# The Overflow branch's copies issued by GpSimd, and four conditioning chunks computed by GpSimd and ScalarE

## The chip, the cores and the metric

The kernel runs on one NeuronCore of a Trainium2 chip. The time is that of one execution on the device, in microseconds (us). Five engines run their own instruction queues and meet through semaphores: TensorE (PE in the profile; PEld are its weight loads), VectorE (DVE), ScalarE (ACT), GpSimd (POOL) and SyncE (SP). Sixteen DMA engines move the data; here SyncE issues nearly all loads of weights.

## The reference

One sequence of 256 tokens of width 1024 goes through nine stages: attention, a mixture of experts, a pooling mixer, a second mixture of experts, a final norm, and then four more blocks (mixer_ab, a feed-forward block, mixer_c, a second feed-forward block). All is f32. The first part conditions each layer on one vector `c`:

```python
c_act = silu(c)
for i in range(DEPTH):                       # 2
    mod = c_act @ ada_w[i] + ada_b[i]        # (1024) x (1024, 6144)
    sh_m, sc_m, gt_m, sh_f, sc_f, gt_f = split(mod, 6)
    h = modulate(rmsnorm(x, norm_mix_g[i]), sh_m, sc_m)
    y = fox_attention(h, ...) if i == 0 else pool_mixer(h, ...)
    x = x + gt_m * y
    h = modulate(rmsnorm(x, norm_ffn_g[i]), sh_f, sc_f)
    y = grouped_moe(h, router_w, router_bias, w1[i], w3[i], w2[i])   # 32 experts, 2 per token
    x = x + gt_f * y
```

An expert is `(silu(x @ w1) * (x @ w3)) @ w2` with a hidden width of 512; each token goes to two of 32 experts.

## The kernel before

**Weights.** All large weights come in chunks of 128 x 4096 f32 (2.097 MB). `prefetch` (L206) issues them on SyncE's queue, strictly in the order of a list, each into a slot of one of three rings: ringa with three slots, ringb with four (until the second mixture of experts is done), ringc with three (opened after attention, closed in layer 1's expert loop). A chunk is issued when a slot is free, that is when `free` has been called for the chunk that was in it; on the chip SyncE then waits for the engine that reads that chunk last.

**Conditioning.** The product of `c_act` with `ada_w` is 24 chunks, ADA, of 4 x 1024 x 128 numbers each. The first four and the last four are multiplied by TensorE. The sixteen between, ADA_ROWS = ADA[4:20], are VectorE's, in `ada_cols` (L657): the chunk lies with 128 output columns on the partitions, and for each of its four groups one instruction multiplies 128 x 1024 weights by `crow` (c_act on every partition), adds them up along the row and adds the bias (L663; in the trace it is CUSTOM_DVE_ANT_0 with a READ_ACCUMULATOR behind it). `attention` calls `ada(2)` whenever a weight chunk of its own is used up, so that the chunks are spread over the stage; the loads of attn, ada and wo chunks follow the same order. `gate` and update of the residual x (L761) come at the end of attention.

**Experts.** Each mixture of experts runs over 16 pairs p of experts. Per pair: `up` (64 matmuls of L1190 with four weight chunks), silu and product (L1194, L1197), `turned` (four transposes L1203 and the copy into the tile uT, L1205), `down` (32 matmuls L1217 with two chunks, then the result in two parts into the tiles yh and yl: L1228 and L1229 in layer 0, L1223 to L1226 in layer 1), and `spread_out` (L1237, L1242) of the pair before. `gather` (L1155) fetches the tokens of the next two pairs with the one-hot oh (L1141), and gate products (L1144) follow. A pair has room for 64 tokens of each expert.

**Overflow.** If an expert gets more tokens than that, `overflow` redoes its share with a loop. It is called in both layers at p = 9, between `up` and `turned`, and it is an If on a number that the engines load from `mint` (L1287, L1288). It borrows the buffers hg, oh, uT, yh and yl. In the run shown no expert overflows, so the branch is skipped. The copies within it (one, and 26 in the body of a loop, L1299 to L1325) are issued by ScalarE. Transfers that the hardware queues of SyncE and ScalarE issue are counted on eight semaphores, DMAHW0 to DMAHW7, in turn; those that GpSimd issues on DMASW0 to DMASW7. Where a branch is skipped, the program raises the counts by what the branch would have added.

**What sets the order.** TensorE's order is written out by hand (manual schedule). On the other engines a scheduler orders the instructions by its own estimate of when they are ready.

Of the kernel before, what the change touches and what calls it, by code (L numbers as in the profile page):

```python
# [19 lines left out]
T = 256  # L20
# [19 lines left out]

ADA = [(l, j) for l in range(2) for j in range(12)]
ADA_ROWS = ADA[4:20]

VEC = {}
_n = 0
# [119 lines left out]
class Net:  # L165
# [491 lines left out]
    def ada_cols(self, l, j):  # L657
# [7 lines left out]
        self.free(("ada", l, j))  # L665
        self.ada_done(l, j)

    def ada_mm(self, chunks, row, pp, tags=("pL", 2, "gm", 1)):

        nc = self.nc  # L670
        n = len(chunks)
        pg = pp.tile([128, 512], F32, name=tags[0], bufs=tags[1])
        ws = [self.get(("ada",) + a).rearrange("p (k n) -> p k n", k=KT) for a in chunks]
        for kt in range(KT):
            for i, w in enumerate(ws):
                q = 32 * (kt % 4 if n == 1 else 2 * i + kt % 2)
                nc.tensor.matmul(pg[q:q + 32, :], self.ca[:, kt:kt + 1].to_broadcast([128, 32]), w[:, kt, :], start=kt < 4 // n, stop=kt >= KT - 4 // n)
        for a in chunks:
            self.free(("ada",) + a)
        nc.scalar.copy(row, pg)  # L680

        def turn():
            pm = pp.tile([128, n, 4], F32, name=tags[2], bufs=tags[3])
            for c in range(4):
                nc.tensor.matmul(pm[:, :, c], row[:, c * 128:(c + 1) * 128], self.sel if n == 1 else self.halfsel,
                                 start=True, stop=True)
            for i, (l, j) in enumerate(chunks):
                nc.vector.tensor_tensor(self.mod[l][:, 4 * j:4 * j + 4], pm[:, i, :], self.vec(f"ada_b{l}", 4 * j, 4), op=OP.add)
                self.ada_done(l, j)
        return turn  # L690
# [10 lines left out]
    def attention(self):  # L701
        nc, tc = self.nc, self.tc
        with ExitStack() as es:
# [63 lines left out]

            def ada(n):
                for _ in range(n):
                    self.ada_cols(*todo.pop(0))  # L770

            lo, hi = range(0, 4), range(4, 8)
            qk(0, 0, range(4))
# [504 lines left out]
    def overflow(self, l, htok, gate, slot, mint, cap, yacc, wp, pp):  # L1278


        nc, tc, A = self.nc, self.tc, self.A
        h = wp.tile([128, KT, T], F32, name="hg")
        idr = wp.tile([128, 2, 4, 64], F32R, name="oh").rearrange("p a b n -> p (a b n)")[:, 0:128]
        ug = wp.tile([128, 4, 128], F32, name="uT").rearrange("p a n -> p (a n)")
        u, gr = ug[:, 0:T], ug[:, T:2 * T]
        w, wd = (wp.tile([128, D], F32, name=n) for n in ("yh", "yl"))
        rv = nc.values_load(mint[0:1, 0:1], min_val=0, max_val=T)  # L1287
        with tc.If(rv > cap):  # L1288
            with ExitStack() as es:
                dp = es.enter_context(tc.tile_pool(name=f"ovd{l}", bufs=1, space=DRAM))  # L1290
                rows = dp.tile([NE, T], F32, name="rows")
                nc.scalar.copy(idr, self.ident)
                ov, rsb = w[:, 0:2 * NE].rearrange("p (a e) -> p a e", a=2), wd[0:NE, 0:T]
                nc.vector.scalar_tensor_tensor(ov, slot, float(cap), gate, op0=OP.is_gt, op1=OP.mult)
                pr = pp.tile([NE, T], F32, name="e1", bufs=2)
                for tt in range(2):
                    nc.tensor.transpose(pr[:, tt * 128:(tt + 1) * 128], ov[:, tt, :], self.ident)
                nc.vector.tensor_copy(rsb, pr)
                nc.scalar.dma_start(rows, rsb)  # L1299
                for k in range(KT):  # L1300
                    ph = pp.tile([128, T], F32, name="e1", bufs=2)
                    for tt in range(2):
                        for i in range(2):
                            nc.tensor.matmul(ph[:, tt * 128:(tt + 1) * 128], htok[i][:, tt, k * 128:(k + 1) * 128], idr,
                                             start=i == 0, stop=i == 1)
                    nc.vector.tensor_scalar(h[:, k, :], ph, self.mscale[l][:, 1, k:k + 1], self.shift(l, 1)[:, k:k + 1],
                                            op0=OP.mult, op1=OP.add)
                wk = w.rearrange("p (k n) -> p k n", k=KT)
                we = A["exp"][l].rearrange("q c p (a b n) -> q c p a b n", a=4, b=2)
                with tc.For_i(0, NPAIR, 1) as pv:  # L1310
                    for ab in range(2):
                        src = rows[:, :].rearrange("(q a) t -> q a t", a=2)[ds(pv, 1), ab, :]
                        nc.scalar.dma_start(gr, src.to_broadcast([128, T]))
                        for ft in range(4):
                            ps = []
                            for i in range(2):
                                for c in range(2):
                                    nc.scalar.dma_start(
                                        wk[:, 4 * c:4 * c + 4, :],
                                        we[ds(pv, 1), 2 * i + c, :, :, ab, ft * 128:(ft + 1) * 128]  # L1320
                                        .rearrange("q p a n -> (q p) a n"))
                                ps.append(pp.tile([128, T], F32, name="e0", bufs=2))
                                self.dense(ps[i], wk, 0, h)
                            for hf in range(2):
                                nc.scalar.dma_start(wd[:, 512 * hf:512 * hf + 512],  # L1325
                                                  we[ds(pv, 1), 4 + hf, :, ft, ab, :].rearrange("q p n -> (q p) n"))
                            nc.scalar.activation(u, ps[0], AF.Silu)
                            nc.vector.tensor_tensor(u, u, ps[1], op=OP.mult)
                            nc.vector.tensor_tensor(u, u, gr, op=OP.mult)
                            if l:  # L1330
                                nc.vector.tensor_tensor(wd, wd, self.gb, op=OP.mult)
                                for tt in range(2):
                                    for hf in range(2):
                                        nc.tensor.matmul(yacc[tt][hf], u[:, tt * 128:(tt + 1) * 128], wd[:, 512 * hf:512 * hf + 512],
                                                         start=False, stop=False, skip_group_check=True)
                            else:
                                for nt in range(KT):
                                    nc.tensor.matmul(yacc[:, nt, :], wd[:, nt * 128:(nt + 1) * 128], u,
                                                     start=False, stop=False, skip_group_check=True)
# [1078 lines left out]
```

## Time and profile before

| | us |
|---|---|
| median of 3 runs | 1869.39 |
| lowest and highest | 1868.79, 1871.61 |
| the profiled execution | 1871.96 |
| its span (first to last instruction) | 1870.2 |
| attention, to the last update of x | about 192 |
| mixture of experts of layer 0, to its last `down` | 677.3 |
| mixture of experts of layer 1, to its last `down` | 1186.5 |

The page gives busy times of the engines and the span in 40 slices with the DMA rate. The timeline lists instructions with start, length and, in brackets, the idle time of their engine before them and what ended it: `[5.78 <-SPq L1288]` is a wait of 5.78 us that SyncE's instruction of line 1288 ended. The list of waits adds these up. The windows give busy times, the granted clock of TensorE as a share of 2.4 GHz (PEclk) and the busy share of the DMA engines.

### The profile page before, as it was taken

How to read it: one execution, taken by the hardware profiler on the slowest of the kernel's cores; microseconds unless marked ns; L12 is line 12 of the kernel's file. 1: busy time of each engine (PE TensorE's matmuls, PEld its weight loads, DVE VectorE, ACT ScalarE, POOL GpSimd, SP SyncE). 2: the span in 40 equal slices, each digit the busy share in tenths (PEclk: the TensorE clock that was granted, in tenths of full speed). 3: DMA queues.
4: the chain of work that ended last, by engine and by line, in shares of the span. 5: the costliest groups of instructions: out<-in, count | busy, mean ns of one | idle time of the engine just before them, and what ended most of it. 6: DMA issues, size and time to landing. Idle time of an engine off the chain costs nothing. (4 is left out here: it accounts for less than half of the span.)

```text
span 1870.2 us, 26586 instructions
## 1 busy us (share of the span) xinstructions
PE 1738.4 (93%) x11262; PEld 1165.4 (62%) x11262; DVE 791.0 (42%) x1552; ACT 532.7 (28%) x950; POOL 163.6 (9%) x249
## 2 busy tenths in 40 slices
PE   6998999999589989999995999999999999999998
PEld 4666544443234445444433434779999989989997
DVE  4687422211112125222522242665655566565554
ACT  2321211111001122111200101445644466564443
POOL 0000000000000000000440340223000002200000
PEclk9999999999789999999997999989999999999999
DMA  9998899999999996999996999615344533344531
GB/s 397 426 422 317 366 427 427 426 428 426 426 390 426 426 428 273 421 426 410 427 426 273 421 413 426 256 68 193 150 177 180 196 143 136 136 158 181 214 127 66
DMA packets 41665, 582.52 MB, mean 311 GB/s; under 512 B 4625, under 2 KB 4753, under 8 KB 5953
## 3 DMA queue, kind: packets, MB, share of 16 engines
q1 hardware_dynamic: 41328, 580.46, 75.1%
q8 instruction: 92, 1.51, 0.3%
q10 hardware_dynamic: 208, 0.26, 0.1%
q14 instruction: 37, 0.30, 0.0%
HBM read 579.65 MB, written 1.05 MB: 311 GB/s over the span
## 5 line engine op out<-in xcount | busy, mean ns | idle before, releaser
L243 DVE TENSOR_TENSOR wlo<-ringa,whi 128x1024 fp32r<-128x1024 f32 x192 | 228.5, 1231 | 174.6 <-ACT whi L242 174.6
L1190 PE MATMUL e<-ringb,hg 128*64 128x512 f32 x1056 | 233.9, 594 | 1.2 <-DMA ringb<-in_exp 1.2
L242 ACT CAST whi<-ringa 128x1024 fp32r<-128x1024 f32 x192 | 191.4, 1050 | 144.2 <-issue 54.9
L266 PE MATMUL ph<-hlo,whi 128*128 128x256 f32 x704 | 198.8, 282 | 1.2 <-DVE hlo L557 1.2
L265 PE MATMUL ph<-hhi,whi 128*128 128x256 f32 x704 | 198.6, 282 | 0.0
L267 PE MATMUL ph<-hhi,wlo 128*128 128x256 f32 x704 | 198.4, 282 | 0.0
L1197 DVE TENSOR_TENSOR u<-u,e 128x512 f32<-128x512 f32 x32 | 22.0, 688 | 384.1 <-PE e L1190 384.1
L1190 PEld LDWEIGHTS e<-ringb,hg 128*64 128x64 f32 x1056 | 79.6, 137 | 146.2 <-issue 141.8
L1190 PE MATMUL e<-ringa,hg 128*64 128x512 f32 x592 | 134.2, 599 | 17.7 <-DVE yl L1229 16.0
L266 PEld LDWEIGHTS ph<-hlo,whi 128*128 128x128 f32 x704 | 133.9, 190 | 2.4 <-DVE hlo L557 1.6
L265 PEld LDWEIGHTS ph<-hhi,whi 128*128 128x128 f32 x704 | 133.9, 190 | 0.8
L267 PEld LDWEIGHTS ph<-hhi,wlo 128*128 128x128 f32 x704 | 133.9, 190 | 0.0
L1467 POOL TENSOR_TENSOR ringa<-ringa 128x128 f32<-128x128 f32 (+1 forms) x86 | 45.8, 545 | 813.5 <-DVE ringa L1463 703.3
L1217 PE MATMUL e<-ringa,uT 128*64 128x512 f32 x384 | 91.4, 623 | 19.4 <-DVE uT L1205 15.8
L1190 PEld LDWEIGHTS e<-ringa,hg 128*64 128x64 f32 x592 | 45.1, 138 | 100.9 <-issue 81.7
L1217 PE MATMUL e<-ringb,uT 128*64 128x512 f32 x416 | 95.8, 606 | 8.8 <-DVE uT L1205 7.2
L1190 PE MATMUL e<-ringc,hg 128*64 128x512 f32 x400 | 88.4, 592 | 1.8 <-DMA ringc<-in_exp 1.8
L1228 ACT ACTIVATE yh<-e,gs 128x512 fp32r<-128x512 f32 x32 | 21.9, 687 | 226.0 <-PE e L1217 195.3
L1160 ACT ACTIVATE hg<-e,mod,msc 128x256 f32<-128x256 f32 x64 | 36.2, 565 | 164.9 <-DVE hg L1162 157.1
L1224 ACT CAST yh<-u 128x512 fp32r<-128x512 f32 x32 | 19.8, 618 | 217.6 <-DVE u L1223 217.6
L1155 PE MATMUL e<-oh,hth 128*128 128x256 f32 x256 | 68.9, 305 | 12.1 <-DVE oh L1141 7.5
L1229 DVE SCALAR_TENSOR_TENSOR yl<-e,gs,yh 128x512 fp32r<-128x512 f32 x32 | 23.9, 750 | 123.7 <-ACT yh L1228 123.7
(588 smaller groups left out, 3209.5 us busy)
## 6 DMA issues: line engine op xcount, KB each, us to landing
ringb<-in_exp SPq DMA_DIRECT2D x92, 2048.0 KB, 20.0
ringa<-in_exp SPq DMA_DIRECT2D x61, 2048.0 KB, 19.7
ringc<-in_exp SPq DMA_DIRECT2D x39, 2048.0 KB, 24.0
ringa<-in_f SPq DMA_DIRECT2D x32, 2048.0 KB, 7.5
ringb<-in_ada SPq DMA_DIRECT2D x15, 2048.0 KB, 16.2
ringa<-in_ada SPq DMA_DIRECT2D x9, 2048.0 KB, 21.9
ringa<-in_cin SPq DMA_DIRECT2D x8, 2048.0 KB, 7.4
ringa<-in_attn SPq DMA_DIRECT2D x3, 2048.0 KB, 28.2
```

The costliest lines, as they stand in the source:

```text
L242: nc.scalar.copy(hi[:, o], raw[:, o])
L243: (eng or nc.vector).tensor_tensor(lo[:, o], raw[:, o], hi[:, o], op=OP.subtract)
L265: mm(ps, wh, ah, start=start, stop=False, **kw)
L266: mm(ps, wh, al, start=False, stop=False, **kw)
L267: mm(ps, wl, ah, start=False, stop=stop, **kw)
L1155: nc.tensor.matmul(pd[:, i, :], htok[h][:, tt, k * 128:(k + 1) * 128], oh[:, tt, :], start=tt + h == 0, stop=tt + h == 2)
L1160: nc.scalar.activation(hg[q][:, k, :], pd[:, i, :], AF.Identity, scale=sc[:, k:k + 1], bias=sh[:, k:k + 1])
L1190: nc.tensor.matmul(ps[s, :], h[:, kt, o:o + 64], w[:, k, ab, :], start=kt == 0, stop=kt == KT - 1)
L1197: nc.vector.tensor_tensor(u, u, ph[1], op=OP.mult)
L1217: nc.tensor.matmul(py[s, :], uT[:, ft, s], w[:, ft, ab, :], start=ft == 0, stop=ft == 3)
L1229: nc.vector.scalar_tensor_tensor(lo, py, g, hi, op0=OP.mult, op1=OP.subtract)
L1467: nc.gpsimd.tensor_tensor(o, a, b, op=op)
```

## The change

Two edits. The copies inside `overflow` are issued by GpSimd's queue in place of ScalarE's. And four of VectorE's sixteen conditioning chunks, ADA_POOL = ADA[9:17:2] (numbers 9, 11, 13 and 15), go to a new function: GpSimd multiplies each row by crow in place, ScalarE sums the row along with a copy in place, and GpSimd adds the bias.

```diff
--- before.py
+++ after.py
@@ -40,6 +40,7 @@
 
 ADA = [(l, j) for l in range(2) for j in range(12)]
 ADA_ROWS = ADA[4:20]
+ADA_POOL = ADA[9:17:2]
 
 VEC = {}
 _n = 0
@@ -665,6 +666,18 @@
         self.free(("ada", l, j))
         self.ada_done(l, j)
 
+    def ada_cols2(self, l, j):
+
+        nc = self.nc
+        w = self.get(("ada", l, j)).rearrange("p (n k) -> p n k", n=4)
+        m = self.mod[l][:, 4 * j:4 * j + 4]
+        for n in range(4):
+            nc.gpsimd.tensor_tensor(w[:, n, :], w[:, n, :], self.crow, op=OP.mult)
+            nc.scalar.activation(w[:, n, :], w[:, n, :], AF.Identity, accum_out=m[:, n:n + 1])
+        self.free(("ada", l, j))
+        nc.gpsimd.tensor_tensor(m, m, self.vec(f"ada_b{l}", 4 * j, 4), op=OP.add)
+        self.ada_done(l, j)
+
     def ada_mm(self, chunks, row, pp, tags=("pL", 2, "gm", 1)):
 
         nc = self.nc
@@ -767,7 +780,8 @@
 
             def ada(n):
                 for _ in range(n):
-                    self.ada_cols(*todo.pop(0))
+                    a = todo.pop(0)
+                    (self.ada_cols2 if a in ADA_POOL else self.ada_cols)(*a)
 
             lo, hi = range(0, 4), range(4, 8)
             qk(0, 0, range(4))
@@ -1296,7 +1310,7 @@
                 for tt in range(2):
                     nc.tensor.transpose(pr[:, tt * 128:(tt + 1) * 128], ov[:, tt, :], self.ident)
                 nc.vector.tensor_copy(rsb, pr)
-                nc.scalar.dma_start(rows, rsb)
+                nc.gpsimd.dma_start(rows, rsb)
                 for k in range(KT):
                     ph = pp.tile([128, T], F32, name="e1", bufs=2)
                     for tt in range(2):
@@ -1310,19 +1324,19 @@
                 with tc.For_i(0, NPAIR, 1) as pv:
                     for ab in range(2):
                         src = rows[:, :].rearrange("(q a) t -> q a t", a=2)[ds(pv, 1), ab, :]
-                        nc.scalar.dma_start(gr, src.to_broadcast([128, T]))
+                        nc.gpsimd.dma_start(gr, src.to_broadcast([128, T]))
                         for ft in range(4):
                             ps = []
                             for i in range(2):
                                 for c in range(2):
-                                    nc.scalar.dma_start(
+                                    nc.gpsimd.dma_start(
                                         wk[:, 4 * c:4 * c + 4, :],
                                         we[ds(pv, 1), 2 * i + c, :, :, ab, ft * 128:(ft + 1) * 128]
                                         .rearrange("q p a n -> (q p) a n"))
                                 ps.append(pp.tile([128, T], F32, name="e0", bufs=2))
                                 self.dense(ps[i], wk, 0, h)
                             for hf in range(2):
-                                nc.scalar.dma_start(wd[:, 512 * hf:512 * hf + 512],
+                                nc.gpsimd.dma_start(wd[:, 512 * hf:512 * hf + 512],
                                                   we[ds(pv, 1), 4 + hf, :, ft, ab, :].rearrange("q p n -> (q p) n"))
                             nc.scalar.activation(u, ps[0], AF.Silu)
                             nc.vector.tensor_tensor(u, u, ps[1], op=OP.mult)
```

What moves on the engines. First ScalarE at layer 0's branch, from the hg activations of the next pairs to pair 10's silu; the semaphores that an instruction waits for stand behind it. Before:

```order
L1160 ACTIVATE hg<-e_3055,mod_106,msc_108 128x256 [waits DVE_49]
L1228 ACTIVATE yh<-e_3075,gs 128x512 [waits DMAHW0_49,DMAHW7_49,PE_49,Activation_49]
L1228 ACTIVATE yh<-e_3088,gs 128x512 [waits PE_49]
L1194 ACTIVATE u<-e_3101 128x512 [waits PE_49]
L1228 ACTIVATE yh<-e_3185,gs 128x512 [waits DVE_49,PE_49]
```

and after:

```order
L1174 ACTIVATE hg<-e_3075,mod_106,msc_108 128x256 [waits DVE_49]
L1242 ACTIVATE yh<-e_3095,gs 128x512 [waits DMASW0_49,DMASW7_49,PE_49,Activation_49]
L1242 ACTIVATE yh<-e_3108,gs 128x512 [waits PE_49]
L1208 ACTIVATE u<-e_3121 128x512 [waits PE_49]
L1242 ACTIVATE yh<-e_3205,gs 128x512 [waits DVE_49,PE_49]
```

The order is the same; the first write of yh waits for the software queue's counters in place of the hardware queues'. VectorE at the same place, from the gate products to pair 10's product, before:

```order
L1144 TENSOR_TENSOR oh<-oh,gate 128x256 [waits DVE_49]
L1205 COPY uT<-e_3066 128x512 [waits DMAHW2_49,PE_49]
L1144 TENSOR_TENSOR oh<-oh,gate 128x256 [waits DVE_49]
L1229 SCALAR_TENSOR_TENSOR yl<-e_3075,gs,yh 128x512 [waits DMAHW1_49,DMAHW2_49,DMAHW0_49,Activation_49]
L1229 SCALAR_TENSOR_TENSOR yl<-e_3088,gs,yh 128x512 [waits Activation_49]
```

and after:

```order
L1158 TENSOR_TENSOR oh<-oh,gate 128x256 [waits DVE_49]
L1219 COPY uT<-e_3086 128x512 [waits DMASW2_49,PE_49]
L1158 TENSOR_TENSOR oh<-oh,gate 128x256 [waits DVE_49]
L1243 SCALAR_TENSOR_TENSOR yl<-e_3095,gs,yh 128x512 [waits DMASW1_49,DMASW2_49,DMASW0_49,Activation_49]
L1243 SCALAR_TENSOR_TENSOR yl<-e_3108,gs,yh 128x512 [waits Activation_49]
```

Here too the counters alone are others. GpSimd from the mask at the start to layer 0's branch, before:

```order
L312 TENSOR_SCALAR mask<-jp 128x128 x2
L945 TENSOR_TENSOR rws<-vt,msc_108 128x256
L945 TENSOR_TENSOR rws<-vt,msc_109 128x256
L1287 TENSOR_LOAD mint
L1288 COMPARE_AND_BRANCH
```

and after:

```order
L675 TENSOR_TENSOR ringa<-ringa,crow 128x1024 x4
L678 TENSOR_TENSOR mod_106<-mod_106,vt 128x4
L959 TENSOR_TENSOR rws<-vt,msc_108 128x256
L675 TENSOR_TENSOR ringb<-ringb,crow 128x1024 x4
L678 TENSOR_TENSOR mod_106<-mod_106,vt 128x4
L675 TENSOR_TENSOR ringa<-ringa,crow 128x1024 x4
L678 TENSOR_TENSOR mod_107<-mod_107,vt 128x4
L675 TENSOR_TENSOR ringb<-ringb,crow 128x1024 x4
L678 TENSOR_TENSOR mod_107<-mod_107,vt 128x4
L959 TENSOR_TENSOR rws<-vt,msc_109 128x256
L1301 TENSOR_LOAD mint
L1302 COMPARE_AND_BRANCH
```

Sixteen products and four bias sums stand ahead of the second of the two rws products (the router's weights, scaled). And VectorE at the end of attention, over the last two conditioning chunks, before:

```order
L663 ISA mod_107 128x1
L761 SCALAR_TENSOR_TENSOR x<-pL,mod_106,x 128x256
L663 ISA ringa,mod_107<-ringa,crow,vt 128x1024
L663 ISA mod_107 128x1
L663 ISA ringa,mod_107<-ringa,crow,vt 128x1024
L663 ISA mod_107 128x1
L663 ISA ringa,mod_107<-ringa,crow,vt 128x1024
L663 ISA mod_107 128x1
L761 SCALAR_TENSOR_TENSOR x<-pL,mod_106,x 128x256
L663 ISA ringa,mod_107<-ringa,crow,vt 128x1024
L663 ISA mod_107 128x1
L761 SCALAR_TENSOR_TENSOR x<-pL,mod_106,x 128x256 x4
```

and after:

```order
L664 ISA mod_107 128x1
L774 SCALAR_TENSOR_TENSOR x<-pL,mod_106,x 128x256
L664 ISA ringa,mod_107<-ringa,crow,vt 128x1024
L664 ISA mod_107 128x1
L664 ISA ringa,mod_107<-ringa,crow,vt 128x1024
L664 ISA mod_107 128x1
L664 ISA ringa,mod_107<-ringa,crow,vt 128x1024
L664 ISA mod_107 128x1
L664 ISA ringa,mod_107<-ringa,crow,vt 128x1024
L664 ISA mod_107 128x1
L774 SCALAR_TENSOR_TENSOR x<-pL,mod_106,x 128x256 x4
```

The last chunk's four rows stand in one block, where before an update of x stood between its third and its fourth.

## Rows read from the trace of the kernel before

**Rows 1.** the page: its span, and GB/s moved in its 40 slices

```profile
span 1870.2 us, 26586 instructions
...
GB/s 397 426 422 317 366 427 427 426 428 426 426 390 426 426 428 273 421 426 410 427 426 273 421 413 426 256 68 193 150 177 180 196 143 136 136 158 181 214 127 66
```

**Rows 2.** waits of SyncE, 470 to 560 and 975 to 1060: total, times, longest

```profile
SPq L1288 <- SPq L1288: 38.7, 8, 5.0
...
SPq L1288 <- SPq L1288: 25.2, 1, 25.2
```

**Rows 3.** timeline, layer 0's branch: start, length, engine, line, tiles, idle before

```profile
207.84 0.69 POOL L945 TENSOR_TENSOR rws<-vt,msc 128x256 f32<-128x256 f32 x1 [124.57 <-DVE yh L1087]
471.79 3.65 PE L1190 MATMUL e<-ringb,hg 128*64 128x512 f32 x16 [1.15 <-DMA ringb<-in_exp]
496.54 0.69 DVE L1205 COPY uT<-e 128x512 f32<-128x512 f32 x1 [5.78 <-SPq L1288]
497.29 9.30 PE L1217 MATMUL e<-ringb,uT 128*64 128x512 f32 x32 [7.19 <-DVE uT L1205]
521.01 1.27 ACT L1228 ACTIVATE yh<-e,gs 128x512 fp32r<-128x512 f32 x2 [30.66 <-SPq L1288]
522.54 8.62 PE L1190 MATMUL e<-ringa,hg 128*64 128x512 f32 x32 [15.95 <-DVE yl L1229]
```

**Rows 4.** timeline, layer 1's branch, and the last matmuls of its last `down`

```profile
973.88 3.65 PE L1190 MATMUL e<-ringa,hg 128*64 128x512 f32 x16 [0.17 <-DMA ringa<-in_exp]
1003.60 0.69 DVE L1205 COPY uT<-e 128x512 f32<-128x512 f32 x1 [14.38 <-SPq L1288]
1004.35 6.63 PE L1217 MATMUL e<-ringa,uT 128*64 128x512 f32 x16 [15.78 <-DVE uT L1205]
1010.81 3.60 PE L1217 MATMUL e<-ringb,uT 128*64 128x512 f32 x16
1182.87 3.60 PE L1217 MATMUL e<-ringa,uT 128*64 128x512 f32 x16
```

**Rows 5.** timeline of TensorE, pairs 13 and 15 of layer 0, and its end

```profile
600.61 7.07 PE L1190 MATMUL e<-ringb,hg 128*64 128x512 f32 x32
652.92 7.07 PE L1190 MATMUL e<-ringa,hg 128*64 128x512 f32 x32
670.19 7.09 PE L1217 MATMUL e<-ringc,uT 128*64 128x512 f32 x32
```

**Rows 6.** windows: length, busy us of PE, PEld, DVE, ACT, POOL, PEclk, DMA share, GB/s

```profile
120.00:140.00 20.00, 20.00 (x87) 10.19 (x86) 16.96 (x46) 6.17 (x22) 0.00 (x0) 1.00 1.00 422
500.00:540.00 40.00, 24.05 (x109) 8.70 (x106) 2.10 (x3) 1.86 (x3) 0.00 (x0) 0.76 0.92 383
1000.00:1020.00 20.00, 13.00 (x186) 5.69 (x187) 5.99 (x12) 1.24 (x2) 0.00 (x0) 0.74 0.48 185
```

**Rows 7.** groups by line (last column: busy, mean ns | idle before)

```profile
L663 DVE CUSTOM_DVE_ANT_0 ringb<-ringb,crow,vt 128x1024 f32<-128x1024 f32 x32 | 39.1, 1273 | 0.0
L1911 POOL TENSOR_TENSOR xc<-xc,vt 128x1024 f32<-128x1024 f32 x1 | 2.5, 2455 | 0.0
L242 ACT CAST whi<-ringa 128x1024 fp32r<-128x1024 f32 x192 | 191.4, 1050 | 144.2 <-issue 54.9
```

**Rows 8.** timeline of TensorE at the end of attention: its waits for VectorE

```profile
161.47 3.72 PE L759 MATMUL pL<-oT,ringb 128*128 128x256 f32 x16 [2.34 <-DVE x L761]
169.40 1.13 PE L759 MATMUL pL<-oT,ringb 128*128 128x256 f32 x4 [3.41 <-DVE x L761]
173.41 4.87 PE L759 MATMUL pL<-oT,ringb 128*128 128x256 f32 x12 [2.88 <-DVE x L761]
```

**Rows 9.** timeline around 1244, GpSimd's product and VectorE's scans

```profile
1244.03 2.46 POOL L1911 TENSOR_TENSOR xc<-xc,vt 128x1024 f32<-128x1024 f32 x1
1244.54 2.09 DVE L1711 TENSOR_TENSOR_SCAN wr<-s5mag,wr 128x64 f32<-128x64 f32 x2
1246.87 0.27 DVE L1711 TENSOR_TENSOR_SCAN wr<-s5mag,wr 128x64 f32<-128x64 f32 x1
```

## The prediction

> **What bounds the kernel now.** I read the page first, then busy time by windows, then the waits and the timeline at the two places that the change touches. The span is 1870.2 us [rows 1]; the profiled execution took 1871.96 us, 1.8 us of it outside the span, and the median of the three runs is 1869.39 us, 2.6 us under the profiled one. The sums below are made against the span and then carried to the median. Two limits take turns in the first 1200 us: the weight stream, which moves 426 to 428 GB/s wherever it is not held up [rows 1], and TensorE.
>
> The Overflow branch sits in each layer's expert loop behind the first half of pair 9. It is not taken here, and still costs time. SyncE stands at the branch line for 38.7 us in layer 0 and for 25.2 us in layer 1, released each time by itself, step by step [rows 2]: it raises, one by one, the counters that the skipped copies of the ScalarE queue would have raised, and each raise waits until the earlier loads on that counter have landed. Meanwhile it issues no load, and whoever touches a tile that the branch could have written waits as well. In layer 0 [rows 3] the copy into uT waits 5.78 us for SyncE, TensorE's second half of pair 9 starts 7.19 us late, ScalarE's first write of yh waits 30.66 us for SyncE, and TensorE starts pair 10 at 522.54 us after 15.95 us of waiting. In layer 1 [rows 4] the copy into uT waits 14.38 us and TensorE 15.78 us.
>
> **The change part by part: the copies of the branch.** They move to GpSimd and so to counters of their own (the order rows show uT, yh and yl waiting for DMASW where DMAHW stood). SyncE then has nothing to raise. GpSimd must raise its own counters where the branch is skipped, but no transfer ran on them before, and it comes to layer 0's branch right behind its second rws product, which ran at 207.84 us [rows 3], some 270 us before TensorE does, and to layer 1's behind the products that it makes for the S5 part in pairs before. What stays is each engine's own passage through the branch.
>
> Layer 0. The copy into uT would start 5.8 us earlier, pair 9's second half at 491.5 instead of 497.29, and after its 9.30 us [rows 3] pair 10 at about 501 instead of 522.54. TensorE can't keep all 21.7 us. Two pairs take it 652.92 - 600.61 = 52.31 us [rows 5], 26.2 us each, but a pair needs six chunks of 2.097 MB, 4.91 us each at 427 GB/s, 29.5 us. So it runs into the loads again, three or so pairs before the end. The last chunk of pair 9's first half was in at 471.79, where TensorE began on it as soon as it landed; 38 more chunks follow (two, then six for each of six pairs), the last lands at 471.79 + 38 x 4.91 = 658.4, its 16 matmuls take 3.5, and the layer ends at 661.9. Before it ended at 670.19 + 7.09 = 677.28 [rows 5]. Gain 15.4 us. If the stream still loses what it loses between 500 and 540 now (a DMA share of 0.92 over 40 us, 3.2 us [rows 6]), 12; if the loads were in early enough for TensorE to keep everything, 21.7; the middle one is worked out from this stage's own pace, and I take it.
>
> Behind this layer the router and layer 1's start run with full rings, so the shift is carried along whole.
>
> Layer 1. The first half of pair 9 meets its last load by 0.17 us [rows 4], so the loads are no further ahead there. Without SyncE's steps uT goes 14.4 us earlier, as soon as the gate product in front of it ends. The 32 matmuls of the second half now take from 1004.35 to 1010.81 + 3.60 = 1014.41, 10.06 us, at a granted clock of 0.74 between 1000 and 1020 [rows 6], where the same 32 take 7.09 us at full clock [rows 5]: the clock had been dropped to 1.2 GHz behind the idle stretch. With a gap of about 2 us in its place most of these 3.0 us should come back. 14.4 + 3.0 = 17.4; I take 17. From 1004 on TensorE waits for no load until 1182.87 + 3.60 = 1186.47 [rows 4]. Does that stay so when it starts 17 us earlier? The last of 38 chunks would be in at 973.88 + 38 x 4.91 = 1160.5 and the layer could end at 1164.0; TensorE wants to end at 1169.5. It does, by 5 us. Lower bound 11 (a clock low at the other end, a load that comes late by 3 us), upper 19.
>
> The stretch behind 1187 hangs on TensorE, VectorE and ScalarE handing work to each other, its loads follow TensorE's pace, and nothing of it is edited: shift carried, 0 us.
>
> **The conditioning chunks.** Sixteen of VectorE's multiply-and-sum rows (four chunks of four) leave it, 16 x 1.21 us pitch (1.27 us each [rows 7]) = 19.3 us. Where these stood, TensorE is busy the whole time (20.00 of 20 us [rows 6]): that is cover, and the 19.3 us free nothing by themselves. TensorE waits for VectorE only at the end of attention, 2.34, 3.41 and 2.88 us [rows 8], because the rows of the last four chunks stand between x updates that free TensorE's accumulators. Those four chunks stay on VectorE. In the order rows of after, the last chunk's four stand in one block, where before an update stood between its third and its fourth row: one row, 1.2 us, more ahead of an update that TensorE waits for, and the same once more at the update before if TensorE's place has slipped against VectorE's. I put both, 2 x 1.2 = 2.4 us. The bounds are a gain of 8.6 us (VectorE so far ahead that all three waits go) and the loss below.
>
> GpSimd's price for a 128x1024 product of two tensors is 2.46 us [rows 7], 16 of them 39.4 us; ScalarE's for a 128x1024 pass 1.05 us [rows 7], 16.8 us. GpSimd is idle there. ScalarE's sums stand in its queue ahead of copies and exponentials that TensorE waits for, so a late product holds those too. And the two engines get in each other's way: a pair of small scans on VectorE, 0.27 us for one, took 2.09 us beside GpSimd's 2.46 us product, and ended 0.14 us behind it [rows 9]. A VectorE row with two SBUF inputs that comes upon a running product waits for its end. The moved products meet VectorE's other chunk rows, which have two such inputs. If half of the 16 are met halfway, 8 x 1.2 = 9.8 us, less than the 19.3 taken off; I put 1 us on the path. Attention: 2.4 + 1 = 3.4 us longer. If every product holds VectorE for its whole length, 39.4 - 19.3 = 20.1 us longer. The end of attention is where SyncE's stream takes up again, and TensorE meets loads until pair 9, so the shift is carried.
>
> The Trainium skill says this too: the page "GPSIMD Engine Reference" (sections "Specifications" and "Key points") has GpSimd and VectorE share their SBUF interfaces, with contention for VectorE instructions that have two SBUF inputs. By that rule, taken at its worst, the time would be that of the second rival below; the trace shows the contention [rows 9], but only for single instructions.
>
> **Sum.** 1870.2 - 15.4 - 17 + 3.4 = 1841.2 us of span, 1843.0 for an execution like the profiled one, 1840.4 against the median. Forecast 1840 us, in its own range 1834 to 1848.
>
> **The rivals.** (a) Attention gains: VectorE's 19.3 us put it so far ahead that the three waits vanish. 8.6 us less instead of 3.4 more: 1828. For it: all three are for VectorE [rows 8]. Against: the rows in the tail are as many as before, in larger blocks. Chance 0.10.
>
> (b) Products hold VectorE each time, 20.1 us instead of 3.4: 1857. For it, [rows 9]; against, much of VectorE's work between its chunk rows has one input in PSUM (the score rows, z from pQ), and a product that falls there holds nothing. Chance 0.15.
>
> (c) The change does not take the wait away: the tiles are still held at the branch, now by GpSimd's raising or by the engines' common passage. Only attention's 3.4 us remain: 1873, no change that a measurement tells. Against: GpSimd's counters have nothing in flight. Chance 0.06.
>
> (d) Slower: in attention the products and VectorE's rows take turns, and ScalarE's sums, which wait for each product, hold the copies that TensorE needs. 16 x (2.46 + 1.21) = 58.7 us less the 19.3 taken off is 39.4, more than the 32.4 that the branches give: 1869.4 + 39.4 - 32.4 = 1876. It decides from the point where more than 52 of the 59 us fall on TensorE's path. Against: ScalarE is busy 6.17 of 20 us there [rows 6], and TensorE's work stands between the sums. Chance 0.06.
>
> **How the numbers follow.** 0.63 for the forecast, 0.10, 0.15, 0.06 and 0.06 for the rivals. The range takes in (b) and all but the edge of (a): 1829 to 1857. A difference of under 0.2%, 3.7 us, can't be told from no change. Faster by more than that: 0.63 + 0.10 + 0.15 = 0.88; within: (c), 0.06; slower: (d), 0.06.
>
> **What would show it.** SyncE no longer stands at the branch line; uT's copy comes 1 us behind the gate product in both layers, pair 10 starts 14 to 24 us earlier relative to its pair 9; layer 0's last pairs wait for loads by 3 us a pair again; layer 1's do not. In attention: products of about 2.5 us on GpSimd, VectorE rows beside them longer than 1.28 us, and the three waits of TensorE at the end at about 2.3, 4.6 and 4.1 us. The forecast is wrong if GpSimd or the branch itself appears as releaser of uT or yh, if TensorE shows waits for ScalarE's copies between 60 and 150 us, or if layer 1's second half meets loads.

## The result, and the profile of the changed kernel

The changed kernel takes 1849.29 us (median of four runs, 1847.91 to 1850.1) against 1869.09 us before: a ratio of 0.9892, with a 95% interval from 0.9875 to 0.9909. It is faster by 20 us, where the prediction had 29. The time lies in the wide range of 1829 to 1857 us, but 1.3 us above the forecast's own range of 1834 to 1848: it stands about half way between the forecast and rival (b). The profiled execution of the changed kernel took 1847.91 us, its span is 1846.2 us, 24.0 us under that of before. That is more than the medians differ by, because the profiled execution of before (1871.96 us) was slower than any of its four timed ones and that of after was the fastest of its four; the stage table below adds up to the 24.

Lines of the changed kernel stand 13 or 14 higher than those of before: L1219 is the copy into uT (L1205), L1231 `down` (L1217), L1204 `up` (L1190), L772 and L774 the matmuls and the update of x at the end of attention (L759, L761), L664 VectorE's chunk rows (L663), L675 GpSimd's products.

First the page of the changed kernel:

```profile
span 1846.2 us, 26611 instructions
```

**The branch.** SyncE's waits around layer 0's branch, 480 to 560 us (total, times, longest), the first and the last of five:

```profile
SPq L207 <- DMA ringb<-in_exp: 27.9, 7, 4.7
...
SPq L207 <- DMA ringc<-in_exp: 3.6, 2, 2.5
```

The other three are for loads and matmuls as well. The branch line is not among them; in [rows 2] it stood there with 38.7 us. The timeline of the same place, and then of layer 1's branch:

```profile
482.67 3.65 PE L1204 MATMUL e<-ringb,hg 128*64 128x512 f32 x16 [1.16 <-DMA ringb<-in_exp]
...
501.07 0.68 DVE L1219 COPY uT<-e 128x512 f32<-128x512 f32 x1
...
501.80 7.09 PE L1231 MATMUL e<-ringb,uT 128*64 128x512 f32 x32 [1.75 <-DVE uT L1219]
508.72 7.04 PE L1204 MATMUL e<-ringa,hg 128*64 128x512 f32 x32
...
970.27 3.65 PE L1204 MATMUL e<-ringa,hg 128*64 128x512 f32 x16 [0.39 <-DMA ringa<-in_exp]
...
985.82 0.68 DVE L1219 COPY uT<-e 128x512 f32<-128x512 f32 x1
...
986.56 3.65 PE L1231 MATMUL e<-ringa,uT 128*64 128x512 f32 x16 [1.74 <-DVE uT L1219]
990.04 3.60 PE L1231 MATMUL e<-ringb,uT 128*64 128x512 f32 x16
...
1160.49 3.60 PE L1231 MATMUL e<-ringa,uT 128*64 128x512 f32 x16
```

The copy into uT waits for nobody. From the last 16 `up` matmuls of pair 9 to pair 10 it is 508.72 - 482.67 = 26.05 us in layer 0, where [rows 3] give 522.54 - 471.79 = 50.75: 24.7 us less. In layer 1 the second half starts 986.56 - 970.27 = 16.3 us behind, where [rows 4] give 30.5, and takes 7.08 us in place of 10.06. At the end of layer 0 TensorE meets the loads again; the second half of its last `up` in the changed kernel, and its last `down`:

```profile
655.75 3.65 PE L1204 MATMUL e<-ringb,hg 128*64 128x512 f32 x16 [1.42 <-DMA ringb<-in_exp]
660.55 3.65 PE L1204 MATMUL e<-ringc,hg 128*64 128x512 f32 x16 [1.15 <-DMA ringc<-in_exp]
...
667.56 7.09 PE L1231 MATMUL e<-ringc,uT 128*64 128x512 f32 x32
```

**Attention.** GpSimd's products, VectorE beside them and TensorE, from the timelines of the changed kernel:

```profile
91.54 12.24 POOL L675 TENSOR_TENSOR ringb<-ringb,crow 128x1024 f32<-128x1024 f32 x4
...
92.59 3.36 DVE L664 CUSTOM_DVE_ANT_0 ringb<-ringb,crow,vt 128x1024 f32<-128x1024 f32 x1
...
123.11 9.87 POOL L675 TENSOR_TENSOR ringb<-ringb,crow 128x1024 f32<-128x1024 f32 x4
...
123.23 5.25 DVE L913 TENSOR_TENSOR p<-p,sm 128x256 f32<-128x256 f32 x2
...
136.86 1.03 DVE L913 TENSOR_TENSOR p<-p,sm 128x256 f32<-128x256 f32 x2
...
103.75 7.17 PE L624 MATMUL pL<-h,ringb 128*128 128x256 f32 x32 [1.20 <-ACT qT L748]
129.00 1.12 PE L933 MATMUL pO<-PT,v 128*64 128x256 f32 x4 [4.45 <-DVE PT L925]
169.95 3.73 PE L772 MATMUL pL<-oT,ringb 128*128 128x256 f32 x16 [2.46 <-DVE x L774]
179.62 2.08 PE L772 MATMUL pL<-oT,ringb 128*128 128x256 f32 x4 [4.08 <-DVE x L774]
184.84 3.78 PE L772 MATMUL pL<-oT,ringb 128*128 128x256 f32 x8 [3.14 <-DVE x L774]
195.74 7.15 PE L772 MATMUL pL<-oT,ringb 128*128 128x256 f32 x32
```

A chunk row that takes 1.28 us alone takes 3.36 beside a product. The two instructions that divide the softmax rows by their sums (L913) take 1.03 us at 136.86, where GpSimd is idle, and 5.25 us at 123.23: the two wait for the ends of two products. The copy into PT stands behind them on VectorE, and TensorE waits 4.45 us for it. The last three waits are those of [rows 8], 2.34, 3.41 and 2.88 before.

The stages by both profiles, in us (a stage's end is the end of its last wo matmul or of its last `down`; pair 9 is its fourth group of `up` matmuls):

| point | before | after | shift | change in this stage |
|---|---|---|---|---|
| first wo matmul | 143.62 | 151.98 | +8.4 | +8.4 |
| end of attention | 192.1 | 202.9 | +10.8 | +2.4 |
| end of layer 0's experts | 677.28 | 674.65 | -2.6 | -13.4 |
| pair 9 of layer 1 | 973.88 | 970.27 | -3.6 | -1.0 |
| end of layer 1's experts | 1186.47 | 1164.09 | -22.4 | -18.8 |
| span | 1870.2 | 1846.2 | -24.0 | -1.6 |

### The profile page after: what moved, and what is told of

The parts are those of the page before. It is cut to its first block, busy times and chain, and to the rows that moved or that the text cites. A ratio compares the mean times of both kernels' runs of the same rounds, so it can differ in the third digit from the quotient of the medians.

```text
span 1846.2 us, 26611 instructions
## 1 busy us (share of the span) xinstructions
PE 1732.1 (94%) x11262; PEld 1159.7 (63%) x11262; DVE 787.3 (43%) x1520; ACT 549.3 (30%) x982; POOL 207.8 (11%) x269
## 3 DMA queue, kind: packets, MB, share of 16 engines
HBM read 579.65 MB, written 1.05 MB: 315 GB/s over the span
## 5 line engine op out<-in xcount | busy, mean ns | idle before, releaser
L1204 PE MATMUL e<-ringb,hg 128*64 128x512 f32 x1056 | 234.8, 597 | 6.6 <-DMA ringb<-in_exp 6.6
L1204 PEld LDWEIGHTS e<-ringb,hg 128*64 128x64 f32 x1056 | 79.6, 138 | 153.2 <-issue 144.1
L1204 PE MATMUL e<-ringa,hg 128*64 128x512 f32 x592 | 133.0, 593 | 5.6 <-DMA ringa<-in_exp 5.6
L1204 PEld LDWEIGHTS e<-ringa,hg 128*64 128x64 f32 x592 | 43.9, 137 | 88.9 <-issue 81.6
L1231 PE MATMUL e<-ringb,uT 128*64 128x512 f32 x416 | 93.6, 594 | 3.4 <-DVE uT L1219 1.7
L1231 PE MATMUL e<-ringa,uT 128*64 128x512 f32 x384 | 87.8, 602 | 5.3 <-issue 3.6
L1204 PE MATMUL e<-ringc,hg 128*64 128x512 f32 x400 | 88.6, 593 | 3.8 <-DMA ringc<-in_exp 3.8
L1238 ACT CAST yh<-u 128x512 fp32r<-128x512 f32 x32 | 19.8, 618 | 199.7 <-DVE u L1237 199.7
L1208 ACT ACTIVATE u<-e 128x512 f32<-128x512 f32 x32 | 19.1, 597 | 197.1 <-PE e L1204 197.0
```

Of the source, the lines that this page charges most:

```text
L1204: nc.tensor.matmul(ps[s, :], h[:, kt, o:o + 64], w[:, k, ab, :], start=kt == 0, stop=kt == KT - 1)
L1231: nc.tensor.matmul(py[s, :], uT[:, ft, s], w[:, ft, ab, :], start=ft == 0, stop=ft == 3)
```

## The experiments

The theory after the comparison (A): the edits work against each other. The branch gives 30 us and more, and the conditioning chunks cost all that attention lost, which the later stages don't give back. The rivals: that layer 0's loads had hidden attention's delay (B), that the passage through the branch holds the engines whoever copies (C).

**The branch alone.**

```diff
-                nc.scalar.dma_start(rows, rsb)
+                nc.gpsimd.dma_start(rows, rsb)
-                        nc.scalar.dma_start(gr, src.to_broadcast([128, T]))
+                        nc.gpsimd.dma_start(gr, src.to_broadcast([128, T]))
...
```

(and the same for the copies into wk and wd; `ada_cols2` is left out.)

> Only the branch's copies go to GpSimd; all sixteen conditioning chunks stay on VectorE. Theory A (the two edits work against each other: the branch gives about 33 us, the chunks take back what attention lost, 10.8 us at its end): attention as in the kernel before, TensorE's last wo matmul at about 192; layer 0's second half of pair 9 5.8 us earlier than before, its end, set by the loads, at about 662 in place of 677; layer 1 another 17 to 19 us; 1834 to 1838 us. Theory B (the loads of layer 0 hid attention's delay in the changed kernel, so undoing it gives nothing): 1849, as the changed kernel.

Measured: 1840.17 us, ratio 0.983 (0.981 to 0.9849), 30.8 us under the kernel before on this chip. Attention ends at 192.05, as before. TensorE around layer 0's branch and at the ends of both layers:

```profile
491.84 7.09 PE L1217 MATMUL e<-ringb,uT 128*64 128x512 f32 x32 [1.37 <-DVE uT L1205]
498.76 7.04 PE L1190 MATMUL e<-ringa,hg 128*64 128x512 f32 x32
...
650.00 3.65 PE L1190 MATMUL e<-ringc,hg 128*64 128x512 f32 x16 [1.16 <-DMA ringc<-in_exp]
...
657.00 7.09 PE L1217 MATMUL e<-ringc,uT 128*64 128x512 f32 x32
...
1155.18 3.60 PE L1217 MATMUL e<-ringa,uT 128*64 128x512 f32 x16
```

Layer 0 ends at 664.1, 13.2 us earlier than before; layer 1 at 1158.8, 27.7 earlier. Layer 1 itself gave 14.6 us, where A had 17 to 19 (more on this below). B falls: without the chunks' edit the kernel is 9 us faster than with it. The time is 2 us over what A had expected.

**The chunks alone.**

```diff
+ADA_POOL = ADA[9:17:2]
...
-                    self.ada_cols(*todo.pop(0))
+                    a = todo.pop(0)
+                    (self.ada_cols2 if a in ADA_POOL else self.ada_cols)(*a)
```

> Only the four conditioning chunks move; the branch's copies stay with ScalarE. Theory A: attention ends 10 to 11 us later, TensorE waits 4 to 5 us for the copy into PT once near 129 us and at a lower clock behind it, and nothing later gives it back: 1878 to 1881 us, slower than before by 0.5%. Theory B: the delay is hidden by the loads, 1869 to 1872. The prediction's own term, 3.4 us, would give 1872.5.

Measured: 1881.8 us, ratio 1.0056 (1.0035 to 1.0076): slower by 10.8 us, and 0.8 above what A had expected. The p rows and the wait for PT are the same as in the changed kernel:

```profile
123.15 5.25 DVE L913 TENSOR_TENSOR p<-p,sm 128x256 f32<-128x256 f32 x2
...
128.91 1.12 PE L933 MATMUL pO<-PT,v 128*64 128x256 f32 x4 [4.46 <-DVE PT L925]
```

-30.8 and +10.8 add up to -20.0, and the changed kernel's gain is 19.8: within the spread of the runs (each interval is some 4 us to either side) the two edits simply add up, and the second one is a loss.

**Three copies left with ScalarE.** What makes the branch costly was so far only read off the waits. Here the copy of the rows and the two into gr stay where they were, the 48 others go to GpSimd (the loop's body has 50 copies: for each of two experts one into gr and, four times, four into wk and two into wd; not 26):

```diff
                 nc.scalar.dma_start(rows, rsb)
                         nc.scalar.dma_start(gr, src.to_broadcast([128, T]))
-                                    nc.scalar.dma_start(
+                                    nc.gpsimd.dma_start(
...
```

> As the branch alone, but the copy of the rows and the two copies into gr stay on ScalarE's queue, the others go to GpSimd: SyncE has three counters to raise in each layer in place of eight. Theory A (the cost is SyncE's raises, each waiting for the loads last counted on that semaphore): the three are the oldest of the rotation. In layer 0 SyncE stands at the branch for about 15 us, uT still waits 5 to 6 us for it, but yh waits for nothing of it (no 30 us wait of ScalarE), pair 10 starts about 508, the loads set the end again; in layer 1 the three loads have landed long ago, so uT waits under 1 us. 1834 to 1840 us. Theory C (the passage through the branch itself holds the engines, whoever copies): 1860 to 1870.

Measured: 1839.49 us, ratio 0.9836 (0.9813 to 0.9859), as the branch alone. SyncE's waits at the branch, layer 0 and layer 1, and the instructions that wait for it in layer 0:

```profile
SPq L1288 <- SPq L1288: 14.2, 3, 4.9
...
SPq L1288 <- SPq L1288: 0.7, 2, 0.4
...
497.43 0.69 DVE L1205 COPY uT<-e 128x512 f32<-128x512 f32 x1 [5.18 <-SPq L1288]
...
504.41 0.69 ACT L1228 ACTIVATE yh<-e,gs 128x512 fp32r<-128x512 f32 x1 [12.55 <-PE e L1217]
```

Three raises instead of eight: 14.2 us in layer 0 in steps of up to 4.9, and 0.7 in layer 1, where the raises before took 25.2 [rows 2]. uT still waits for SyncE in layer 0, yh doesn't. Pair 10 starts at 507.58, as expected. So a raise costs as long as the load last counted on that semaphore is under way: in layer 0 the eight waits of before are about one load long each (38.7 us in all, 5.0 at most). In layer 1 before there was one wait of 25.2 us and none behind it; that the first counter in the row was that of the load issued last is inferred from this, and was not tried. C falls. The 14.2 us don't show in the time, since the loads set the end of layer 0.

**The products cut into quarters.** The other side of the balance: is it the length of one product that holds VectorE, or GpSimd's traffic as such?

```diff
-            nc.gpsimd.tensor_tensor(w[:, n, :], w[:, n, :], self.crow, op=OP.mult)
+            for o in range(0, D, 256):
+                nc.gpsimd.tensor_tensor(w[:, n, o:o + 256], w[:, n, o:o + 256], self.crow[:, o:o + 256], op=OP.mult)
```

> The changed kernel with each of GpSimd's products cut into four of 128x256 (about 0.65 us each by the rows of the kernel before). Theory L (a VectorE instruction with two inputs in SBUF waits for the end of the product that is running, and GpSimd for VectorE's): no VectorE row beside products takes more than about 0.7 us over its own length; the p rows that took 5.25 us at 123 take under 3, the wait of TensorE for PT near 129 us, 4.45, goes, and with it the low clock behind it; the first wo matmul starts at 144 to 147 in place of 152; 1840 to 1845 us. Theory S (the two engines share a rate, so that the product's total time counts, however it is cut): the p rows stay at 4 to 5 us, 1848 to 1851. The order of VectorE and ScalarE differs in places, since the scheduler takes four instructions for longer than one.

Measured: 1845.41 us, ratio 0.9855 (0.983 to 0.988). GpSimd's groups, the longest p rows of the stage, TensorE's waits and the first wo matmul:

```profile
L676 POOL TENSOR_TENSOR ringb<-ringb,crow 128x256 f32<-128x256 f32 x32 | 24.9, 812 | 0.0
...
124.69 2.02 DVE L914 TENSOR_TENSOR p<-p,sm 128x256 f32<-128x256 f32 x2
...
122.29 3.70 PE L760 MATMUL pL<-ringa,h 128*128 128x512 f32 x8 [2.33 <-ACT kT L749]
127.24 0.65 PE L934 MATMUL pO<-PT,v 128*64 128x256 f32 x4 [1.25 <-DVE PT L926]
...
145.91 3.72 PE L773 MATMUL pL<-oT,ringb 128*128 128x256 f32 x16
```

GpSimd works longer in all than with whole products (the four chunks take 47.7 us in place of 41.3), and yet the p rows take 2.02 us in place of 5.25, TensorE's wait for PT falls from 4.45 to 1.25, the granted clock between 120 and 140 us is 1.00, and the first wo matmul starts 6.1 us earlier. So at the p rows it is the length of the single product that counts, and not the sum (L, against S). But L does not hold everywhere. In the same run VectorE was held through several quarters in a row:

```profile
113.35 3.56 DVE L909 TENSOR_SCALAR mx<-mx 128x2 f32<-128x2 f32 x1
...
116.83 4.05 DVE L664 CUSTOM_DVE_ANT_0 ringb<-ringb,crow,vt 128x1024 f32<-128x1024 f32 x1
...
121.00 0.40 ACT L911 ACTIVATE p<-z,mx 128x128 f32<-128x128 f32 x1 [3.00 <-DVE mx L909]
```

GpSimd's quarters ran there without a gap until 116.89 and again from 117.00 to 119.78; the first instruction ended with the first stretch of quarters, and the second 1.1 us (a little less than its own length) behind the other. Why VectorE got in between quarters at 124 us and not here stays open. The new wait of 2.33 us for a copy of kT comes from it: the copy stands in ScalarE's queue behind an exponential that waits 3.00 us for VectorE's second maximum. Attention ends at 194.87, 2.8 us later than before. The time itself, 1845.4, is 0.4 us above what L had expected, and its interval touches the changed kernel's.

**The last four chunks instead.** Chunks 16 to 19, those between the x updates, go to GpSimd in place of 9, 11, 13 and 15, once with whole products and once in quarters:

```diff
-ADA_POOL = ADA[9:17:2]
+ADA_POOL = ADA[16:20]
```

> The changed kernel, with the last four of VectorE's chunks (16 to 19) moved in place of 9, 11, 13 and 15. Theory A (products cost where they meet the softmax rows; the chunk rows cost where they stand between x updates): the three waits of TensorE for x at the end of attention, 8.6 us in the kernel before, go, and the products meet only the last heads' rows; attention ends at 184 to 188. But the slots of these four chunks are freed later, by 16 products of 2.5 us behind the arrival of the chunks, so the loads may resume up to 10 us later. 1828 to 1845 us. Theory D (the slots held by GpSimd cost more than the gaps): 1845 to 1860.

> The last four chunks on GpSimd, in quarters as well. Theory L: the wait for PT at 152 us, 5.0 in the run with whole products, goes; what is left is a wait for a late wo chunk (6.3 there). 1838 to 1844 us. Theory S: as with whole products, 1847 to 1850.

Measured: 1848.3 us whole (0.9873, 0.9857 to 0.989) and 1837.76 us in quarters (0.9829, 0.9804 to 0.9854). TensorE's longest waits with whole products, then the longest in quarters:

```profile
152.20 1.12 PE L933 MATMUL pO<-PT,v 128*64 128x256 f32 x4 [5.01 <-DVE PT L925]
...
183.45 5.90 PE L772 MATMUL pL<-oT,ringb 128*128 128x256 f32 x16 [6.34 <-DMA ringb<-in_wo]
```

```profile
172.39 6.55 PE L773 MATMUL pL<-oT,ringb 128*128 128x256 f32 x16 [6.83 <-DMA ringb<-in_wo]
```

Whole products hold the softmax rows here too (5.01 us for PT), quarters don't. In both, a new wait appears for the second wo chunk: the load comes late. That GpSimd empties the slots later than VectorE did is the likely reason; it was not tried apart. Attention ends at 203.2 with whole products, where A had 184 to 188, and the time is in D's range. In quarters it ends at 192.7, 0.7 us later than before, so even the best place for the products gives attention nothing. The time in quarters is just under what L had expected.

**VectorE's last rows later.** The branch alone, with the last two chunks held back behind the x updates of the second wo chunk's first half:

```diff
-            with tc.issue_after(self.last_p):
+            with tc.issue_after(self.last_x):
                 ada(2)
```

(`last_x` is the x update issued last.)

> The branch alone, and VectorE's last two chunks held until the eighth update of the second wo chunk's first half has been issued: the two blocks of four rows no longer stand between x updates that TensorE waits for. Theory A (the attention tail costs what VectorE's rows put between the updates, and a shift of attention's end is carried through layer 0 because the loads resume with it): two of the three waits (3.41 and 2.88) go, attention ends at about 186 in place of 192; 1834 to 1837 us. Theory E (the loads resume when the chunks' slots are freed, and the rows now free them some 10 us later): attention ends earlier but the loads don't resume earlier, 1839 to 1845.

Measured: 1838.82 us, ratio 0.9824 (0.9798 to 0.9851), not to be told from the branch alone. The waits of 3.41 and 2.88 us did not go, they moved:

```profile
182.72 6.93 PE L759 MATMUL pL<-oT,ringb 128*128 128x256 f32 x24 [6.20 <-DVE x L761]
```

The eight rows stand in one block ahead of the next update, and 6.20 is nearly 3.41 + 2.88 = 6.29. Attention ends at 189.65, 2.4 us earlier than in the branch alone, but 1.7 of these were there already at the first wo matmul (141.87 against 143.59). What the edit did to the tail is 0.7 us, so neither expectation is borne out, and which of the tail's end or the slots sets the time stays open.

**Once more on one chip**, to tell three of them apart:

> The changed kernel once more, on the same chip as the next two, to tell them apart by less than half a per cent. Theory A and L: 1848 to 1851 us, 8 to 10 us above the branch alone.

> The branch alone once more. Theory A: 1838 to 1842 us. If the chunks cost nothing that a measurement can tell: the same as the changed kernel.

> The last four chunks on GpSimd in quarters, once more. The first look put it 2.4 us below the branch alone, within the spread. If it is a gain: 1835 to 1838 us and an interval below that of the branch alone; else 1838 to 1842, the same.

Measured: the changed kernel 1853.32 us, ratio 0.99 (0.9882 to 0.9918); the branch alone 1843.09, 0.9849 (0.9834 to 0.9863); the last four in quarters 1837.6, 0.9821 (0.9805 to 0.9837). The first two times are 2.3 and 1.1 us above what was expected of them; the changed kernel is 10 us above the branch alone, with intervals well apart. On this chip the branch alone gave 27.2 us, where it gave 30.8 on the other. The last four in quarters are faster than the kernel before and the changed one. Against the branch alone they are ahead by 5.5 us here and by 2.4 in the first runs, on two chips, with intervals that touch or overlap, and their five times spread from 1836.53 to 1847.1: a gain over the branch alone is not shown.

## Why the prediction was right, and where it was off

**The branch's copies: right in mechanism and near in size.** Predicted 15.4 + 17 = 32.4 us; alone it gave 30.8 and, once more, 27.2. That the first comes so near is in part luck: by the profiles of the first run 13.2 + 14.6 = 27.8 us lie in the two layers, and another 2.7 behind layer 1, where nothing is edited. SyncE's stand at the branch line is gone, uT follows the gate product at once in both layers, the loads bound the end of layer 0 again and (but for one wait of 0.76 us in the branch alone) not that of layer 1, as the prediction had said, and the three-copies run shows that it is SyncE's raises.

Layer 0 gave 13.4 us (13.2 alone), not 15.4. Two things were off. The last of 38 chunks plus its 16 matmuls was taken for the end. The load that binds is the fourth of pair 15's `up`, 36 chunks on: 471.79 + 36 x 4.91 = 648.6. Behind it come its matmuls, silu, the transposes and the whole `down`: 14.1 us in the branch-alone run, from 650.00 to 664.09. Worked out in that way, the end is 662.7, 0.8 us behind the prediction's 661.9; and the load itself was 1.4 us late against that pace in the run.

Layer 1 gave 18.8 us, not 17, in the changed kernel, and 14.6 in the branch alone (from 960.77, where pair 9's last `up` matmuls start, to 1158.78, against 212.6 us before). The two are no different kernels here: once more, the changed kernel gave 16.9 (970.44 to 1166.16) and the branch alone 16.7 (959.41 to 1155.27), so this is a spread from run to run. Of the 4.2 us between the two first runs, 2.9 arise around pair 10's first `up` matmuls, which the branch alone ran in part at the lower clock (its granted clock between 980 and 1000 us is 0.83), and 0.9 at one load that came late. The `up` matmuls of the changed kernel, then the same of the branch alone, and the load:

```profile
1001.05 10.52 PE L1204 MATMUL e<-ringb,hg 128*64 128x512 f32 x48
```

```profile
992.99 12.33 PE L1190 MATMUL e<-ringb,hg 128*64 128x512 f32 x48
...
1108.56 3.65 PE L1190 MATMUL e<-ringa,hg 128*64 128x512 f32 x16 [0.76 <-DMA ringa<-in_exp]
```

Why the clock was low there in one run stays open. All four lie within the bounds of 11 to 19.

**The conditioning chunks: the term that was mis-sized.** Predicted 3.4 us longer, 2.4 for the tail and 1 for the contention; measured 10.8, and 10.7 in the run of the chunks alone (its last wo matmul ended at 202.80). The tail came out at 2.4 us, but by luck: the three waits grew by 1.05 us in all (2.46, 4.08 and 3.14, where the prediction's signs were 2.3, 4.6 and 4.1), and the rest is matmuls at the lower clock between and behind the second and the third of them (four took 2.08 us in place of 1.13). The 1 us is what failed; it was 8.4. The prediction weighed products that are met by chunk rows against the time that VectorE was relieved of. That balance is an average, and what decided was one place: the two p rows at 123 us, which were not in the sum at all. They have two inputs in SBUF as well, the copy into PT stands right behind them, and TensorE waits for that. The four freed chunks had stood where VectorE's time cost nothing, so what was taken off there could not pay for it. The clock behind the longer wait:

```profile
120.00:140.00 20.00, 15.55 (x51) 7.64 (x49) 11.71 (x24) 6.26 (x21) 11.08 (x5) 0.74 0.81 325
...
133.28 6.16 PE L759 MATMUL pL<-ringa,h 128*128 128x512 f32 x8
...
141.64 3.70 PE L759 MATMUL pL<-ringa,h 128*128 128x512 f32 x8
```

The window 120 to 140 of the changed kernel has a granted clock of 0.74, where [rows 6] had 1.00. Eight matmuls took 6.16 us where they ran for the most part at the lower level, 1.2 GHz (0.58 over these 6 us), and 3.70 at 2.4 GHz. The sum can be made from where TensorE stands against the kernel before. At 73 us, ahead of the first product, it is 1.9 us early: its matmuls from 34 us on ran at full clock, where the granted clock of before was 0.91 between 20 and 40 us. What brings this head start stays open: all four traces in which these chunks moved have it, but so has the branch alone with its last rows held back, which moves none. Then the changed kernel loses 1.4 us up to 104 (the wait of 1.20), 0.1 up to 121, 4.5 at the wait for PT, and 4.3 in the matmuls behind it, from 129.00 to 141.64 in place of 124.94 to 133.28. 10.3 lost less 1.9 ahead is 8.4. So the products cost attention some 10 us up to the first wo matmul, and the head start hid two of them. The two rows, of ScalarE's first copy into v, before and after:

```profile
75.26 0.59 ACT L748 COPY v<-pL 128x512 f32<-128x512 f32 x1 [2.79 <-PE pL L746]
...
73.32 0.58 ACT L761 COPY v<-pL 128x512 f32<-128x512 f32 x1 [2.79 <-PE pL L759]
```

**The rivals.** Rival (b), that products hold VectorE, happened in half: the mechanism is its own, at 7.4 us over the forecast in place of 16.7, and through the softmax rows, which the prediction had not named. One of the prediction's signs of being wrong did appear: TensorE waits 1.20 us for ScalarE's copy of qT at 103.75. It is not rival (d), though, since no sum stands ahead of that copy: four exponentials do, and they had waited for VectorE's maxima, which stand behind chunk rows of 3.36 us and were themselves held by a product:

```profile
101.58 0.40 ACT L910 ACTIVATE p<-z,mx 128x128 f32<-128x128 f32 x1 [8.85 <-DVE mx L908]
```

Rival (c) is out: no tile waits at the branch in the changed kernel. Nothing of (a) came. The shift of attention's end was carried to pair 9 of layer 0, as predicted: it stood at 482.67, 10.9 us later. Over the other runs it is the same, from 2.4 us earlier (pair 9 at 469.46, 2.3 earlier) to 11.1 later (483.06, 11.3 later).

The Trainium skill's page "GPSIMD Engine Reference", sections "Specifications" and "Key points", has contention with VectorE instructions of two SBUF inputs or in a two-port mode; the trace agrees (1.03 to 5.25 us and 1.28 to 3.36 us). The prediction read it as a weight on the chunk rows alone; the p rows are such instructions too.

**What lies between.** The prediction set the stretches behind the layers at 0; they gave 1.0 and 1.6 us. Neither is more than the spread of the runs: over the twelve traces the stretch from the end of layer 0 to pair 9 of layer 1 takes 293.6 to 296.7 us, and that behind layer 1 takes 680.8 to 685.2, with no order by edit. What makes these differ was not tried.

## What to carry to other kernels

A branch that is not taken was not free here: whoever stands in for its transfers has to wait for the transfers in flight on the same counters, and everything that shares a tile with the branch waits too, so issue such copies on a queue that carries nothing else at that time. Work moved from VectorE to GpSimd should be weighed at each place where a VectorE instruction with two SBUF inputs is on somebody's path, not by busy time; time that VectorE is relieved of where TensorE is the bound pays for nothing. Where two edits stand in one change, run each alone: here one gave some 30 us and the other took back 10 to 11.

## What the runs showed of the hardware

Beside whole products (2.4 us each when alone), VectorE's instructions with two SBUF inputs were held to the end of a product and then took about their own length. With products a quarter as long the wait of the p rows shrank from 4.2 us (5.25 - 1.03) to 1.0 (2.02 - 1.03), but in another place of that run two instructions were held through five and four quarters in a row (3.56 and 4.05 us), so short instructions do not bound the wait. GpSimd is held as well: four products took 12.24 us beside chunk rows, and 9.32 from 109.01 on, where one chunk row stood beside them. The contention also reaches tiny instructions with one SBUF input. The pair that negates 128x2 maxima, beside a product and with GpSimd idle in its wait for ScalarE, both in the changed kernel:

```profile
80.47 2.52 DVE L908 TENSOR_SCALAR mx<-mx 128x2 f32<-128x2 f32 x2
...
86.32 0.28 DVE L908 TENSOR_SCALAR mx<-mx 128x2 f32<-128x2 f32 x2
```

And one wait of 4.45 us on TensorE was followed by a low clock that cost about as much again, 4.3 us.
